# Three feed-forwards that multiply x before its norm's factor is known, with two covered tiles in place of four

## The chip, the cores and the metric

The kernel runs on one core of a Trainium2 chip. The time is that of one execution on the device in microseconds; the number given for a kernel is the median of its runs. Engines: TensorE (PE; its weight loads are listed as PEld), VectorE (DVE), ScalarE (ACT), GpSimd (POOL) and SyncE (SP). DMAs are issued from SP's queue and from POOL's; those of POOL can add what they carry onto what is in the target.

## The reference

A residual stream x of 512 tokens and 1024 features goes through two layers of three parts, each behind an RMS norm:

```python
for l in range(DEPTH):                                   # 2
    x = x + 0.5 * swiglu(rms_norm(x, ffn1_norm[l]), ffn1_w_in[l], ffn1_w_out[l])
    h = rms_norm(x, mix_norm[l]) @ w_mix_in[l]
    ...                                                  # convolution, HGRN2 and FoX heads give y
    x = x + y @ w_mix_out[l]
    x = x + 0.5 * swiglu(rms_norm(x, ffn2_norm[l]), ffn2_w_in[l], ffn2_w_out[l])

def rms_norm(x, gain):
    inv = lax.rsqrt(jnp.mean(x * x, axis=-1, keepdims=True) + EPS)
    return (x * inv) * gain

def swiglu(h, w_in, w_out):
    gate, up = jnp.split(h @ w_in, 2, axis=-1)           # D_FF = 2816 each
    return (jax.nn.silu(gate) * up) @ w_out
```

So there are four feed-forwards, two in each layer. All is float32.

## The kernel before

x is kept transposed (`xT`, 8 tiles of 128 features by 512 tokens), so that the norm's factor `inv` of a token is a row of 512 values, the same on all partitions.

**Three passes a product.** Every matmul takes float32 operands split into a high part (a cast to fp32r on ScalarE) and a low part (the difference, on VectorE): high by high, high by low, low by high (`mm3`, L357, L365, L366). Weights are split the same way in `prepare` (L832 the cast, L834 the subtraction) or, in a plain stream, granule by granule (L343, L344).

**Two ways to a feed-forward's first projection.** The 22 tiles of 128 columns of gate and up are done partly plainly and partly by halves. Plainly: a pair of tiles is four jobs over 8 tiles of features, 96 matmuls of 512 columns. By halves: a unit `("I", w)` of a pair of tiles, w its first, takes 7 products P1 to P7 of sums of halves (24 matmuls of 256 columns each) in place of 8. Products are combined from their PSUM banks: g1, g2 (gate, by halves of the tokens), u2 and the rest (up). `("O", ...)` units do the second projection in the same way, and T the last two tiles. `covered` tells how many tiles are plain: 6 in the first feed-forward (`FIRST`), 4 in the other three.

**What covers what.** While a plain pair runs, the halves are made ready: `enter` (L586) opens the three later feed-forwards. It runs the plain stream of pair 0 on x times the gain (`xh`, `xl`, without `inv`, which multiplies the result later: `clear`), then the norm's matmul (L476) and, on ScalarE, Ln, Exp and Square with a table load behind (L306, L297). Then comes the plain pair 2, and under it the four quarters of x by gain and `inv` (`quarter`, L622, VectorE), the sums of quarters (L645), and their high and low parts (L635, L638, L640).

**The order of the work.** `plan()` writes out the sequence of products (`ORDER_IN` for units of the first projection) and, for each step, the loads of raw weights (SP's queue), the sums of raw weights and the preparation of moving halves. A product's weights are split `LEAD` = 3 products ahead. Four raw tiles of a unit give the weights of seven products; the sums among them are S2 and S3. A sum of two raw tiles is made either by VectorE (`total`) or by a DMA from POOL's queue that adds another tile from DRAM (`add`, L805), or adds the tile S (`add_second`, L860). In the first unit S3 is a VectorE subtraction and the loads, four at first, are issued at L914. Most instructions keep the order in which they are written on their engine, so one that waits holds all behind it.

**The end of the unit.** ScalarE copies a product's bank into SBUF or into another bank, on which later products add: the copy of P1 (L1036), u (L1048), the copy of P6.

## Time and profile before

| | |
|---|---|
| median of 2 runs | 1796.3 us (1795.2 to 1797.4) |
| profiled execution | 1798.4 us, span 1796.6 us |
| TensorE busy | 1787.1 us (99%) |
| VectorE busy | 1493.2 us (83%) |
| ScalarE busy | 1028.0 us (57%) |
| GpSimd busy | 177.3 us (10%) |
| DMA queue of SP (q1) / of POOL (q0) | 182.38 MB, 33.6% / 69.23 MB, 24.0% of 16 engines' span |

The span is the time from the first to the last instruction that the profile shows; the execution's time is a little more. Busy times overlap: TensorE is the engine that hardly ever idles. A row of a timeline begins with the start and the duration in microseconds, then the engine, the line of the kernel, the operation, what it writes and reads, and in brackets the idle time of the engine before it with what ended it.

### The profile page before, as it was taken

Reading aid. Unit: us, or ns where it says so; the run is one execution under the profiler, and the core shown is the slowest. Engines: PE = TensorE matmul, PEld = TensorE weight load, DVE = VectorE, ACT = ScalarE, POOL = GpSimd, SP = SyncE. Lnnn points to the kernel's source line nnn. Section 1 sums busy time; section 2 is a strip of 40 time slices with the busy share of each in tenths; the row PEclk is TensorE's granted clock in tenths of the full one; section 3 lists DMA queues with packets and bytes.
Section 4 is the critical chain, followed back from the end, with each engine's and each line's share of the span. In section 5 each row is a group of like instructions: output and inputs, shape, how many; then the busy total and the mean of one; then the engine's idle time right before and its main releaser. Section 6 shows DMA issues by size and latency. Waiting matters only on the chain.

```text
span 1796.6 us, 35740 instructions
## 1 busy us (share of the span) xinstructions
PE 1787.1 (99%) x14703; PEld 1695.0 (94%) x14703; DVE 1493.2 (83%) x2098; ACT 1028.0 (57%) x1495; POOL 177.3 (10%) x184
## 2 busy tenths in 40 slices
PE   9999999999999999999999999999999999999999
PEld 7899999999888899999989999998998888999998
DVE  8889788876888798879889787997868778888887
ACT  5455555664776465555646555566547755655553
POOL 0002110100000002112001111101000000020110
PEclk9999999999999999999999999999999999999999
DMA  6659685233433857868266786843334346587682
GB/s 199 176 126 195 172 171 149 54 84 84 107 99 108 224 127 169 196 153 185 74 199 133 172 179 166 185 95 77 78 81 114 90 137 168 142 179 197 141 200 71
DMA packets 242083, 254.15 MB, mean 141 GB/s; under 512 B 18904, under 2 KB 224480, under 8 KB 241920
## 3 DMA queue, kind: packets, MB, share of 16 engines
q1 hardware_dynamic: 189424, 182.38, 33.6%
q0 software_dynamic: 52192, 69.23, 24.0%
q8 instruction: 115, 1.88, 0.4%
q14 instruction: 48, 0.39, 0.1%
q10 hardware_dynamic: 304, 0.27, 0.0%
HBM read 221.88 MB, written 2.10 MB: 125 GB/s over the span
## 4 chain that ended last, share of the span: by engine, by line
PE 91%; DVE 4%; DMA 2%; ACT 2%; issue 1%; SPq 0%; POOL 0%; ACTq 0%; POOLq 0%; DVEq 0%
PE mm L357 13%; PE mm L365 13%; PE mm L366 13%; PE pt L365 6%; PE pt L357 6%; PE pt L366 6%; PE sc L365 6%; PE sc L357 6%; PE sc L366 6%; PE po L365 3%; PE po L357 3%; PE po L366 3%; PE po L1770 1%; PE pt L1814 1%; DMA w<-in_ffn_w_out_dram 1%
## 5 line engine op out<-in xcount | busy, mean ns | idle before, releaser
L832 ACT CAST hl<-w 128x1024 fp32r<-128x1024 f32 x354 | 370.7, 1050 | 367.1 <-PE mm L366 97.3
L834 DVE TENSOR_TENSOR hl<-w,hl 128x1024 fp32r<-128x1024 f32 x354 | 430.9, 1220 | 105.2 <-ACT hl L832 104.0
L357 PE MATMUL mm<-xc,hl 128*128 128x256 f32 (+1 forms) x717 | 197.2, 276 | 0.0
L365 PE MATMUL mm<-xc,hl 128*128 128x256 f32 x712 | 197.1, 277 | 0.0
L366 PE MATMUL mm<-xc,hl 128*128 128x256 f32 x712 | 196.9, 277 | 0.0
L344 DVE TENSOR_TENSOR hl<-st,hl 128x512 fp32r<-128x512 f32 (+2 forms) x172 | 133.0, 774 | 62.9 <-ACT hl L343 62.0
L343 ACT CAST hl<-st 128x512 fp32r<-128x512 f32 (+2 forms) x172 | 117.7, 687 | 102.2 <-PE mm L366 43.4
L357 PE MATMUL pt<-xc,hl 128*128 128x256 f32 x514 | 141.4, 276 | 0.0
L365 PE MATMUL pt<-xc,hl 128*128 128x256 f32 x512 | 141.4, 276 | 0.0
L366 PE MATMUL pt<-xc,hl 128*128 128x256 f32 x512 | 141.3, 276 | 0.0
L357 PE MATMUL sc<-xc,hl 128*128 128x256 f32 (+1 forms) x500 | 137.2, 276 | 0.0
L365 PE MATMUL sc<-xc,hl 128*128 128x256 f32 x496 | 137.1, 276 | 0.0
L366 PE MATMUL sc<-xc,hl 128*128 128x256 f32 x496 | 136.9, 276 | 0.0
L357 PEld LDWEIGHTS mm<-xc,hl 128*128 128x128 f32 x717 | 134.6, 188 | 0.2
L366 PEld LDWEIGHTS mm<-xc,hl 128*128 128x128 f32 x712 | 133.7, 188 | 0.0
L365 PEld LDWEIGHTS mm<-xc,hl 128*128 128x128 f32 x712 | 133.7, 188 | 0.0
L365 PE MATMUL mm<-m,hl 128*128 128x256 f32 x416 | 115.0, 277 | 0.0
L357 PE MATMUL mm<-m,hl 128*128 128x256 f32 x416 | 114.8, 276 | 0.0
L366 PE MATMUL mm<-m,hl 128*128 128x256 f32 x416 | 114.8, 276 | 0.0
L357 PE MATMUL mm<-x,hl 128*128 128x512 f32 x272 | 107.7, 396 | 0.0
L365 PE MATMUL mm<-x,hl 128*128 128x512 f32 x272 | 106.3, 391 | 0.0
L366 PE MATMUL mm<-x,hl 128*128 128x512 f32 x272 | 106.2, 390 | 0.0
(529 smaller groups left out, 5781.8 us busy)
## 6 DMA issues: line engine op xcount, KB each, us to landing
w<-in_ffn_w_in_dram SPq DMA_DIRECT2D x140, 512.0 KB, 4.9
w<-in_ffn_w_out_dram SPq DMA_DIRECT2D x88, 512.0 KB, 4.5
w<-in_ffn_w_out_dram POOLq DMA_DIRECT2D x52, 512.0 KB, 7.3
st<-in_w_mix_in_dram SPq DMA_DIRECT2D x88, 256.0 KB, 2.7
w<-S POOLq DMA_DIRECT2D x39, 512.0 KB, 4.8
st<-in_ffn_w_in_dram SPq DMA_DIRECT2D x70, 256.0 KB, 3.3
w<-in_ffn_w_in_dram POOLq DMA_DIRECT2D x35, 512.0 KB, 8.4
st<-in_w_mix_out_dram SPq DMA_DIRECT2D x20, 256.0 KB, 2.7
```

The source lines that it names most:

```text
L343: a = nc.scalar.copy(hi, src[:, c : c + w])
L344: b = nc.vector.tensor_sub(lo, src[:, c : c + w], hi)
L357: i = nc.tensor.matmul(acc[:, c], ah, bh[:, c], start=first and c.start == 0, stop=False, skip_group_check=True,)
L365: nc.tensor.matmul(acc, a, b, start=False, stop=False, skip_group_check=True)
L366: i = nc.tensor.matmul(acc, c, d, start=False, stop=last, skip_group_check=True)
L832: A(nc.scalar.copy(hi, src))
L834: return lambda: V(nc.vector.tensor_sub(lo, src, hi))
L1770: nc.tensor.matmul(self.ob[:, t0 + u * P : t0 + 2 * P], V[:, j, h % 4].rearrange("p a d -> p (a d)"), part[:, j, u:, :].rearrange("p i t - ...
L1814: nc.tensor.transpose(tb[:, j * P : (j + 1) * P], p[:, j * P : (j + 1) * P], self.ident)
```

## The change

In the three later feed-forwards `inv` is no longer part of x's halves.

- `enter` makes the quarters as x times the gain alone (ScalarE, four pieces of 128x256 a quarter). P1, P2 and P3 take the parts `xh`, `xl` that the norm has made anyway; P5, P6, P7 and P4 need sums of quarters ("four sums of x"). Signs of some copies and P1's weights change with it.
- The second covered pair is gone (`COVERED` = 2): a unit of seven products takes its place.
- `inv` multiplies the gate before its Silu (new VectorE products L1084, L1101), and the residual takes the ratio 1/inv: `ratio` (L684), four multiplications of xT at products 14, 16, 18 and 20 (`rescale`), undone in layer 1's mixer (`UNSCALE`, four multiplications) or taken along by the next norm's bias (L694, a ScalarE square) and, at the end of the kernel, by a `column` factor at the output.
- `ORDER_IN` is P1, P5, P6, P2, P7, P3, P4 in all four feed-forwards. S2 is summed in place. S3 of the later units is taken by VectorE only where P7 comes under 4 steps behind P6; else two DMAs add raw tiles from DRAM (0,2 and 2,1) for P7 and P3. The loads of the first unit come in the order 2, 0, 1, 3, the next ones directly behind. Raw tiles and granules get other buffers (`staged`).

```diff
-ORDER_IN = ("P1", "P2", "P6", "P5", "P7", "P3", "P4")
+ORDER_IN = ("P1", "P5", "P6", "P2", "P7", "P3", "P4")
-FIRST = 6
+FIRST, COVERED = 6, 2
...
             if w == covered:
-                when(-1, 6, "adds", u)
-                when(0, 2, "total", u, "S3")
                 continue
+            begin[2] = split["P5"] - AHEAD_SUM - AHEAD_LOAD
+            when(split["P5"] - AHEAD_SUM, 5, "add", u, 2, 3)
+            between(split["P5"], split["P6"] - 1, "total", u, "S2")
+            if split["P7"] - split["P6"] < 4:
+                begin[3] = split["P6"] - AHEAD_LOAD
+                when(split["P6"], 3, "total", u, "S3")
             else:
...
+                when(split["P6"], 4, "add", u, 0, 2)
+            when(split["P6"], 5, "add", u, 2, 1)
...
-        next(second)
-        self.end_norm(nb, fp, parts, True)
...
-                V(nc.vector.scalar_tensor_tensor(
-                    out=t[:, k, :], in0=self.xT[:, i, b * H : (b + 1) * H],
-                    scalar=(self.gain if a == b else self.ngain)[:, i : i + 1],
-                    in1=self.inv[:, b * H : (b + 1) * H], op0=ALU.mult, op1=ALU.mult,
+                A(nc.scalar.activation(
+                    t[:, k, :], self.xT[:, i, b * H : (b + 1) * H], AF.Copy,
+                    scale=(self.gain if a == b else self.ngain)[:, i : i + 1],
                 ))
...
         quarter(0, 0)
-        high("P1")
-        quarter(1, 0)
-        lows["P1"]()
...
         quarter(0, 1)
...
+        add((0, 0), (0, 1))
+        self.end_norm(nb, fp, parts, True)
+        self.table(SILU)
+        next(first, None)
+        high("P5")
         quarter(1, 1)
+        self.given["first"]()
         lows["P5"]()
...
         add((0, 0), (1, 1))
         high("P6")
+        self.given["second"]()
         lows["P6"]()
+        V(nc.vector.scalar_tensor_tensor(out=ratio, in0=nb, ..., in1=self.inv, ...))
...
+        quarter(1, 0)
         next(then)
...
+            0: lambda: (add((0, 1), (1, 1)), both("P7")),
+            1: lambda: (add((0, 0), (1, 0)), high("P4")),
+            2: lambda: lows["P4"](),
+            7: lambda: clear(0),
...
+            14: lambda: rescale(0, 0),
+            16: lambda: rescale(1, 1),
+            18: lambda: rescale(0, 1),
+            20: lambda: rescale(1, 0),
...
+        def first():
+            prepare(*seq[0])()
+
+        def second():
+            prepare(*seq[1])()
+            total(u, "S2")
+            add(u, 0, 2)
```

How the rows stand on the engines at the places where TensorE's first products come from. The first is ScalarE from the norm's last operation on, in layer 0's second feed-forward. Before (`xc` are the high parts of x's halves, `hl<-st` those of the plain pair's weights, `hl<-w` those of the products' weights, `gi` the plain pair's gate):

```order
L306 ACTIVATE nt_7096<-nr_7095 128x512
L297 ACT_TABLE_LOAD
L635 ACTIVATE xc_7143<-xn_7138 128x1024
L343 CAST hl_7179<-st_7176 128x1024
L635 CAST xc_7182<-xn_7146 128x1024
L343 CAST hl_7223<-st_7220 128x1024
L635 CAST xc_7227<-xn_7138 128x1024
L306 ACTIVATE gi_7230<-gi_7230 128x512
L343 CAST hl_7263<-st_7260 128x1024
L635 CAST xc_7291<-xn_7138 128x1024
L832 CAST hl_7297<-w_7131 128x1024
```

All of these but the last stand beside the plain pair's matmuls. Now, at the same place, up to P1's bank (`mm_7161<-mm_7160` is its copy; `w_7057` are P1's raw weights, `w_7054` those of P5 and, summed, P6, `w_7059` those of P2):

```order
L297 ACT_TABLE_LOAD
L641 CAST xc_7123<-xn_7076 128x1024
L629 ACTIVATE xn_7126<-xT,gain_5590 128x256 x4
L863 ACTIVATE hl_7131<-w_7057 128x1024
L641 CAST xc_7136<-xn_7076 128x1024
L863 CAST hl_7139<-w_7054 128x1024
L694 ACTIVATE sqa_7147<-ratio_7145 128x512
L629 ACTIVATE xn_7149<-xT,ngain_7074 128x256 x4
L863 CAST hl_7156<-w_7054 128x1024
L863 CAST hl_7187<-w_7059 128x1024
L1080 ACTIVATE mm_7161<-mm_7160 128x512
```

The weights' casts, which stood at the end of a plain pair, now stand directly behind the table load, between pieces of x, and the copy of P1's bank stands behind the casts for P6 and P2. VectorE at the same place, now, from the norm's factor `inv` on (`hl` are the weights' low parts, of P1, P5, P6, P2 and P7 in this order; `w_7054<-w_7054,w_7057` is S2):

```order
L865 SCALAR_TENSOR_TENSOR hl_7131<-w_7057,hl_7131 128x1024
L646 TENSOR_TENSOR xc_7124<-xn_7076,xc_7123 128x1024
L651 TENSOR_TENSOR xn_7076<-xn_7076,xn_7126 128x1024
L867 TENSOR_TENSOR hl_7139<-w_7054,hl_7139 128x1024
L847 TENSOR_TENSOR w_7054<-w_7054,w_7057 128x1024
L646 TENSOR_TENSOR xc_7137<-xn_7076,xc_7136 128x1024
L684 SCALAR_TENSOR_TENSOR ratio_7145<-po_7073,inv_7093 128x512
L867 TENSOR_TENSOR hl_7156<-w_7054,hl_7156 128x1024
L867 TENSOR_TENSOR hl_7187<-w_7059,hl_7187 128x1024
L651 TENSOR_TENSOR xn_7081<-xn_7081,xn_7126 128x1024
L644 SCALAR_TENSOR_TENSOR xc_7195<-xn_7081,xc_7194 128x1024
L867 TENSOR_TENSOR hl_7223<-w_7057,hl_7223 128x1024
```

Before, four quarters (L622) and granules' low parts (L344) stood here, ahead of the products' weights; now the low parts of x and of weights take turns with the sums of x. The third place is POOL's queue in the same feed-forward, where units of the first and of the second projection alternate (products 75 to 79 of the change's sequence; `in` and `out` in the names tell the projection). Before:

```order
L860 DMA w_9355<-S_9474 128x1024
L805 DMA w_9058<-in_ffn_w_out_dram 128x4x256
L805 DMA w_9188<-in_ffn_w_out_dram 128x4x256
L805 DMA w_9118<-in_ffn_w_out_dram 128x4x256
L805 DMA w_9290<-in_ffn_w_out_dram 128x4x256
```

Now:

```order
L835 DMA w_9375<-in_ffn_w_in_dram 128x4x256
L835 DMA w_9112<-in_ffn_w_out_dram 128x4x256
L835 DMA w_9278<-in_ffn_w_in_dram 128x4x256
L835 DMA w_9243<-in_ffn_w_out_dram 128x4x256
L835 DMA w_9173<-in_ffn_w_out_dram 128x4x256
L835 DMA w_9345<-in_ffn_w_out_dram 128x4x256
```

The add from the tile S is gone here, and the unit of the first projection takes two adds from DRAM (for P7 and for P3) that stand directly among those of the second projection.

## The prediction

> **What bounds the kernel now.** I began with the page: the head, the busy shares and the chain that ended last.

> ```profile
> span 1796.6 us, 35740 instructions
> PE 1787.1 (99%) x14703; PEld 1695.0 (94%) x14703; DVE 1493.2 (83%) x2098; ACT 1028.0 (57%) x1495; POOL 177.3 (10%) x184
> PE 91%; DVE 4%; DMA 2%; ACT 2%; issue 1%; SPq 0%; POOL 0%; ACTq 0%; POOLq 0%; DVEq 0%
> ```

> TensorE is busy for 99% of the span and makes 91% of the chain, so every matmul removed is time removed, as long as TensorE still waits for nobody. How little it waits now is the next view, TensorE's waits by releaser (8 rows, the first and the last):

> ```profile
> PE pt L1814 <- DVE QA L1716: 1.3, 2, 0.6
> ...
> PE po L476 <- ACT sh L467: 0.2, 1, 0.2
> ```

> The eight rows sum to under 6 us, and none has a product of a feed-forward's first unit. Whatever the change adds as a wait is new loss. The third view is the stretch that the change rewrites, here in layer 0's second feed-forward: first the second covered pair, then the seven products of the first unit (columns: PE, PEld, DVE, ACT, POOL busy; clock; DMA share; GB/s).

> ```profile
> 599.58:621.34 21.76, 21.76 (x98) 18.02 (x97) 21.52 (x30) 10.01 (x11) 1.09 (x2) 1.00 0.75 221
> 621.36:640.41 19.05, 19.05 (x170) 19.05 (x169) 17.11 (x19) 12.14 (x14) 1.10 (x1) 1.00 0.55 112
> ```

> In the covered pair VectorE works 21.52 of 21.76 us. That is the making of x's normed halves, their high and low parts and the sums, all under matmuls that don't need them. The change takes that cover away: what VectorE and ScalarE must do between the norm and the first products decides.

> **What is removed and added on TensorE.** A covered pair is 96 matmuls of 512 columns, 21.76 us by the first window; a unit is 168 of 256 columns, 19.05 us by the second (2.72 a product of 24). Each of the three feed-forwards gains 21.76 − 19.05 = 2.71 us; three make **−8.1 us**. This is all that the change can give.

> **What the first products then wait for.** Times are on the clock of this execution. Nothing ahead of the norm's sum is later than now, by the order of the rows: the two pieces of x scaled there take up idle time of ScalarE (4.86 us ahead of the norm's Ln). Timeline of TensorE, ScalarE and VectorE at this place:

> ```profile
> 593.65 0.62 PE L476 MATMUL po<-sh,ones_mean 128*128 128x512 f32 x2
> 599.58 0.39 PE L357 MATMUL mm<-x,hl 128*128 128x512 f32 x1
> 594.32 0.69 ACT L306 ACTIVATE nr<-po,epsc 128x512 f32<-128x512 f32 x1 [4.86 <-PE po L476]
> 596.35 1.28 ACT L297 ACT_TABLE_LOAD   x1
> 599.99 1.06 ACT L635 ACTIVATE xc<-xn 128x1024 fp32r<-128x1024 f32 x1 [2.35 <-DVE xn L622]
> 616.32 1.99 ACT L832 CAST hl<-w 128x1024 fp32r<-128x1024 f32 x2
> 597.55 0.69 DVE L462 TENSOR_TENSOR inv<-nr,nt 128x512 f32<-128x512 f32 x1
> 601.46 1.22 DVE L638 SCALAR_TENSOR_TENSOR xc<-xn,xc 128x1024 fp32r<-128x1024 f32 x1
> 602.59 1.22 DVE L344 TENSOR_TENSOR hl<-st,hl 128x1024 fp32r<-128x1024 f32 x1
> ```

> The norm's sum ends at 594.27, the first pair's last matmuls run until 599.58, and there P1 is now due. ScalarE is free for it only after the table load, at 597.63. A pass over 128x1024 costs ScalarE 1.05 us, 0.95 where one follows another (1.99 for two); VectorE 1.22, or 1.13 (601.46 to 602.59); the group rows of the weights' two passes, quoted next, have the same over 354 each (1050 and 1220 ns). A quarter of x is now four ScalarE pieces of 128x256, which have no row of this line; the nearest are the first three here; behind them are x's sums and the weights' casts and subtractions:

> ```profile
> L1758 ACT ACTIVATE P<-P,rs 128x256 f32<-128x256 f32 x16 | 8.2, 510 | 3.4 <-DVE rs L1756 3.4
> 570.72 0.71 ACT L437 ACTIVATE x<-xT,gain 128x512 fp32r<-128x512 f32 x1
> 571.34 0.62 ACT L453 ACTIVATE sq<-xT 128x512 f32<-128x512 f32 x1
> L645 DVE TENSOR_TENSOR xn<-xn,xn 128x1024 f32<-128x1024 f32 x12 | 14.6, 1216 | 0.0
> L832 ACT CAST hl<-w 128x1024 fp32r<-128x1024 f32 x354 | 370.7, 1050 | 367.1 <-PE mm L366 97.3
> L834 DVE TENSOR_TENSOR hl<-w,hl 128x1024 fp32r<-128x1024 f32 x354 | 430.9, 1220 | 105.2 <-ACT hl L832 104.0
> ```

> A piece is bounded by 0.51 (single, 128x256) and 0.31 (half the 0.62 pitch of 128x512); I take 0.41, so 1.64 a quarter. Both ends move an entry by under 1 us. Now the changed rows, in the order shown above, each engine taking its rows in turn:

> - ScalarE: high part of P5's x to 598.6, quarter (1,1) to 600.2, P1's weights to 601.3. VectorE: their low part to 602.5. **P1** is due at 599.58 and has two matmuls that need high parts alone; it stands 2.7 us and ends at 605.05.
> - VectorE: low part of P5's x to 603.7, the sum for P6 to 604.8. ScalarE: P6's x to 605.9, and only behind it P5's weights, to 606.8. VectorE: their low part to 608.1. **P5** stands 2.8 us and ends at 610.6.
> - VectorE: weight sum 609.2, low part of P6's x 610.4, ratio 611.0. ScalarE: square of the ratio 611.6, quarter (1,0) 613.2, P6's weights 614.2, P2's weights 615.2, and then the copy of P1's bank, which P1 left ten microseconds earlier, 615.7. P6 adds onto that copy. **P6** stands 5.1 us and ends at 618.4. P2 follows without a wait to 621.1.
> - VectorE: low parts of P6's and P2's weights to 616.6, the sum for P7 617.75. ScalarE: P7's x 618.8, P7's weights 619.8, u 620.3. VectorE: both low parts, the sum for P4 to 622.4. ScalarE: P4's x 623.5, and then the copy of P6's bank, 623.95, on which P7 adds. **P7** stands 2.9 us and ends at 626.7; P3 and P4 follow to 632.1.

> Without a wait the unit would end at 599.58 + 19.05 = 618.6: **13.5 us of waits**. In the last feed-forward there is no square and quarter (1,0) isn't behind the ratio, which brings the copies forward: 10.4. Two entries by 13.5 and one by 10.4 make **+37.4 us**. In the units behind, VectorE has 44 us of work, by the same durations, for 18 products of 2.72 (49 us): by the order's rows it keeps up, but nothing wins the waits back, since TensorE is the bound.

> **The loads.** P5's and P6's weights come out of a DMA that adds one tile onto another.

> ```profile
> 592.64 1.37 POOL L805 DMA_DIRECT2D w<-in_ffn_w_in_dram  x1 [58.27 <-DMA w<-in_ffn_w_in_dram]
> w<-in_ffn_w_in_dram POOLq DMA_DIRECT2D x35, 512.0 KB, 8.4
> q0 software_dynamic: 52192, 69.23, 24.0%
> w<-S POOLq DMA_DIRECT2D x39, 512.0 KB, 4.8
> ```

> Issued at 592.64 and landed 8.4 us later, this sum is there at 601.0, ahead of its cast (from 605.9). The loads that are now issued without a wait don't set the end. All four feed-forwards now take S3 by two such adds instead of a VectorE subtraction and an add from a tile. Where units of both projections meet, six adds follow one another within four products (third order extract above). The queue moved 69.23 MB in 24.0% of the span: 0.524 MB in 3.3 us. The fifth add is needed 9 products (24.5 us) later by a weight that takes 1.05 + 1.22 us: 5 × 3.3 + 2.3 = 18.8, in time. By 4.8 each (the row of adds from S) it is 26.3, 1.8 late, 7 us over four feed-forwards; by 8.4 each, one after another, 44.3, some 20 late each, 80. The row of the queue's own time is nearest: I take +2, keep 0 and 7 in the range, and leave the far end to a rival.

> **Small edits.** The sixteen VectorE multiplications of x by a ratio cost some 1.2 us each; idle VectorE (17% of the span) hides them. Uncovered they would be 20 us, too; I take 0, since products 14 to 20 have a free step each. The column factor at the end replaces copies by scaled copies: 0.

> **Sum.** −8.1 + 37.4 + 2 = +31.3 us on the profiled execution (1798.4 us, span 1796.6) gives 1829.7. The median of the runs, 1796.3, is 2.1 lower: **1828 us**, +1.7%. A measurement of this kernel tells from no change about 2%, 1832.2 on this side and 1760.4 on the other.

> **Rivals.**

> *The clock.* TensorE starts at half rate, and at the end no wait is long enough to show whether a pause brings that back:

> ```profile
> 5.55 1.22 PE L1962 MATMUL sc<-x,hl 128*128 128x512 f32 x2
> 6.57 1.05 PE L1962 MATMUL pt<-x,hl 128*128 128x512 f32 x2
> ```

> Two matmuls of 512 columns take 1.05 to 1.22 here and 0.62 at 593.65. If the 5.1 us before P6 lowers the clock, P6 and part of P2 run at double length, 2.7 to 5.4 more, of which P7's wait hides up to 2.9: +2.6 an entry at the most likely, 8 in all, and 1836. [...]

> *Queue late.* With the adds one after another at the far end the time passes 1850; half of it gives 1868. Against it: the queue's own 3.3 us. With the clock both get 0.17, 1834 to 1850 and beyond.

> *The chain is shorter.* If ScalarE's pieces and hand-offs let P5's and P6's waits overlap (a bank's copy done while VectorE still sums), 4 to 8 us an entry remain: 1796.3 − 8.1 + 2 + 3 × (4 to 8) = 1802 to 1814. 0.17.

> *Not slower: the weights' high parts don't stand behind the norm.* P1's and P5's raw weights are there before 601; if their casts and the bank copies found ScalarE free as soon as their inputs are, only VectorE's row would be left, and the order of x's sums would fit beneath P1 to P6. It decides at 2.7 us of waits an entry, a fifth of my sum: then 1788 to 1797. For it: ScalarE idles 4.86 us ahead of the norm. Against it: the rows put each cast behind the table load. 0.06. That the change doesn't do what it says would need matmuls of 512 columns in those places; the order has them gone.

> **How the numbers follow.** Forecast 0.60, its own range 1818 to 1836 (pieces, hand-offs, 0 to 7 for the queue). A quarter of it, 0.14, lies over 1832.2, with the clock and queue 0.31 slower; nothing reaches 1760, 0.01; the rest is within 2%. The range of 8 in 10 goes from 1806 to 1843: it leaves out the not-slower case, the low part of the shorter chain and the late queue.

> **What will show it.** Right: TensorE's waits gain rows at the first unit of three feed-forwards with releasers VectorE (weights' low parts) for P1 and P5, and ScalarE (copies) for P6 and P7, of some 2.7, 2.8, 5.1 and 2.9 us; 288 matmuls of 512 columns fewer, 504 of 256 more; a granted clock of 1.00 in the unit. Wrong: waits at products 80 to 90 on a DMA (queue), rows of 256 columns at twice 0.11 us behind P6's wait (clock), or a unit that takes 19 to 22 us from the last plain matmul to its seventh product (short chain).

## The result, and the profile after

The changed kernel takes 1880.1 us (two runs, 1878.1 and 1882.0) against 1796.3: a ratio of 1.047 (95% interval 1.041 to 1.052). The profiled execution took 1882.0 us, 83.6 more than that of before. From the page, the head, the busy shares and the chain that ended last:

```profile
span 1880.3 us, 36231 instructions
PE 1815.3 (97%) x14919; PEld 1728.0 (92%) x14919; DVE 1509.3 (80%) x2075; ACT 1054.9 (56%) x1554; POOL 212.5 (11%) x202
PE 80%; DVE 8%; ACT 4%; DMA 4%; issue 2%; SPq 0%; ACTq 0%; POOLq 0%; DVEq 0%
```

TensorE no longer makes nine tenths of the chain. Its waits by releaser, which summed to under 6 us, begin now with these rows (engine, line, releaser, us in all, times, longest):

```profile
PE mm L361 <- ACT g L1090: 15.4, 3, 5.5
PE po L361 <- ACT g L1090: 13.4, 3, 5.0
PE mm L361 <- ACT mm L1080: 9.5, 3, 4.6
PE mm L361 <- ACT hl L863: 6.3, 5, 1.6
PE mm L361 <- ACT g L1063: 5.0, 3, 3.5
PE mm L370 <- DVE hl L867: 2.4, 4, 0.8
```

The last four lie in the first unit of the three feed-forwards, where waits were forecast. The first two, the largest, were not forecast: L1090 is the copy of P6's bank in the units behind the first. The windows of the three units of each of the three feed-forwards show how much each takes (its length in us, then busy time of PE, PEld, DVE, ACT, POOL, the granted clock, DMA share, GB/s); without a wait a unit takes 19.05:

```profile
600.54:633.64 33.10, 25.02 (x170) 23.81 (x170) 22.37 (x22) 17.23 (x24) 3.87 (x3) 0.85 0.63 144
633.64:659.77 26.13, 21.63 (x171) 21.43 (x169) 17.03 (x20) 11.22 (x15) 2.58 (x2) 0.87 0.53 121
659.77:686.54 26.77, 22.08 (x171) 21.88 (x170) 17.91 (x21) 9.99 (x12) 2.59 (x2) 0.87 0.51 119
952.57:986.41 33.84, 25.36 (x171) 24.04 (x170) 23.16 (x23) 17.23 (x24) 3.88 (x3) 0.85 0.63 142
986.41:1011.70 25.29, 21.36 (x171) 21.16 (x169) 16.93 (x20) 11.24 (x15) 2.59 (x2) 0.93 0.56 126
1011.70:1038.71 27.01, 21.55 (x170) 21.35 (x169) 17.64 (x21) 9.74 (x12) 2.59 (x2) 0.87 0.52 117
1542.33:1574.15 31.82, 24.26 (x170) 23.08 (x170) 23.16 (x22) 17.14 (x23) 3.89 (x3) 0.89 0.60 144
1574.15:1601.28 27.13, 22.13 (x171) 21.93 (x169) 17.03 (x22) 11.01 (x14) 2.58 (x2) 0.87 0.53 117
1601.28:1628.59 27.31, 22.10 (x171) 21.91 (x170) 18.50 (x21) 10.06 (x13) 2.59 (x2) 0.88 0.52 116
```

The first units sum to 98.8 us, 41.6 over 3 × 19.05. The second and third ones sum to 159.6, 45.3 over 6 × 19.05. With the 8.1 us that the removed pairs give, 41.6 + 45.3 − 8.1 = 78.8 of the 83.6 us. Of the rest 1.3 us is a longer wait on VectorE near the end (2.16 us in place of 0.87), and 1.1 the half clock behind it.

**What P7 waits for in the second unit.** Timelines of TensorE, ScalarE, VectorE, POOL and SP's queue:

```profile
649.18 0.58 PE L361 MATMUL po<-xc,hl 128*128 128x256 f32 x1 [4.50 <-ACT g L1090]
649.57 0.41 PE L369 MATMUL po<-xc,hl 128*128 128x256 f32 x1
642.37 0.59 ACT L1093 ACTIVATE u<-mm 128x512 f32<-128x512 f32 x1
647.59 1.04 ACT L863 CAST hl<-w 128x1024 fp32r<-128x1024 f32 x1 [4.63 <-DMA w<-in_ffn_w_in_dram]
648.54 0.59 ACT L1090 ACTIVATE g<-po 128x512 f32<-128x512 f32 x1
637.90 1.22 DVE L847 TENSOR_TENSOR w<-w,w 128x1024 f32<-128x1024 f32 x1
639.66 2.58 POOL L835 DMA_DIRECT2D w<-in_ffn_w_in_dram  x2 [20.22 <-DVE w L847]
640.28 10.01 SPq L832 DMA_DIRECT2D w<-in_ffn_w_in_dram  x3
```

Read backwards: P7 adds onto P6's bank, which ScalarE has to copy away first (648.54). The copy stands behind the cast of P3's weights (647.59), and that cast waits 4.63 us for a DMA: the add of a raw tile onto S2. POOL issues it at 639.66, as soon as VectorE's difference for P7 (L847) has read the tile, beside loads on SP's queue, and it lands 7.9 us later.

**The clock.** The matmuls at 649.57 start 0.21 us apart, twice the 0.113 (19.05 over 168) of before. The granted clock changes in steps of 3.41 us; these are some of the windows (length, PE busy, granted clock, DMA share, GB/s):

```profile
599.48:602.89 3.41, 1.83 (x9) 1.00 1.14 289
602.89:606.31 3.42, 2.81 (x13) 0.50 1.09 384
606.31:609.72 3.41, 3.22 (x15) 0.50 1.03 319
609.72:613.13 3.41, 2.48 (x22) 1.00 0.12 13
951.05:954.47 3.42, 1.98 (x11) 1.00 1.17 237
954.47:957.88 3.41, 2.76 (x24) 1.00 1.09 369
643.85:647.27 3.42, 0.83 (x8) 1.00 1.21 200
647.27:650.68 3.41, 1.50 (x7) 0.50 1.17 236
650.68:654.09 3.41, 3.41 (x18) 0.50 0.76 236
654.09:657.50 3.41, 3.41 (x31) 1.00 0.35 122
```

After 1.6 us of idling in one window (599.48) the next two are granted half the clock; after 2.6 (643.85) two again; after 1.4 (951.05) none. Over the whole execution matmuls of 256 columns under half clock take 27.8 us more than at full clock, against 0 before. P7 of the second and third units takes 5.1 to 5.3 us in five of the six cases and 4.5 in the other, in place of 2.7: of the 45.3 us, 30 are waits and 15 the half clock.

### The profile page after: what moved, and what is told of

Read it like the earlier page. It is cut to its first block, busy times and chain, and to the rows that moved or that the text cites. A ratio compares the mean times of both kernels' runs of the same rounds, so it can differ in the third digit from the quotient of the medians.

```text
span 1880.3 us, 36231 instructions
## 1 busy us (share of the span) xinstructions
PE 1815.3 (97%) x14919; PEld 1728.0 (92%) x14919; DVE 1509.3 (80%) x2075; ACT 1054.9 (56%) x1554; POOL 212.5 (11%) x202
## 4 chain that ended last, share of the span: by engine, by line
PE 80%; DVE 8%; ACT 4%; DMA 4%; issue 2%; SPq 0%; ACTq 0%; POOLq 0%; DVEq 0%
PE mm L361 14%; PE mm L369 14%; PE mm L370 14%; PE pt L369 4%; PE pt L370 4%; PE pt L361 4%; PE sc L361 4%; PE sc L370 4%; PE sc L369 4%; DMA w<-in_ffn_w_in_dram 4%; PE po L361 3%; PE po L370 3%; PE po L369 3%; DVE hl L867 2%; DVE w L847 1%
## 5 line engine op out<-in xcount | busy, mean ns | idle before, releaser
L863 ACT CAST hl<-w 128x1024 fp32r<-128x1024 f32 x380 | 397.7, 1050 | 425.5 <-PE mm L370 103.1
L867 DVE TENSOR_TENSOR hl<-w,hl 128x1024 fp32r<-128x1024 f32 x380 | 462.1, 1222 | 160.3 <-ACT hl L863 159.5
L361 PE MATMUL mm<-xc,hl 128*128 128x256 f32 (+1 forms) x1090 | 309.5, 284 | 31.7 <-ACT g L1090 15.4
L370 PE MATMUL mm<-xc,hl 128*128 128x256 f32 x1088 | 308.0, 283 | 2.4 <-DVE hl L867 2.4
L369 PE MATMUL mm<-xc,hl 128*128 128x256 f32 x1088 | 307.5, 283 | 0.0
L361 PEld LDWEIGHTS mm<-xc,hl 128*128 128x128 f32 x1090 | 211.3, 194 | 34.6 <-ACT g L1090 15.9
L361 PE MATMUL mm<-x,hl 128*128 128x256 f32 (+2 forms) x761 | 235.7, 312 | 4.5 <-ACT hl L863 4.5
L370 PE MATMUL mm<-x,hl 128*128 128x256 f32 (+1 forms) x752 | 233.4, 310 | 2.0 <-DVE hl L865 2.0
L369 PE MATMUL mm<-x,hl 128*128 128x256 f32 (+1 forms) x752 | 233.5, 310 | 0.0
L835 POOL DMA_DIRECT2D w<-in_ffn_w_in_dram x88 | 113.9, 1403 | 936.3 <-DVE w L847 254.0
L370 PEld LDWEIGHTS mm<-xc,hl 128*128 128x128 f32 x1088 | 211.0, 194 | 3.4 <-DVE hl L867 3.4
L369 PEld LDWEIGHTS mm<-xc,hl 128*128 128x128 f32 x1088 | 211.3, 194 | 0.0
L347 ACT CAST hl<-st 128x512 fp32r<-128x512 f32 (+2 forms) x160 | 105.2, 660 | 96.3 <-PE mm L370 45.0
L361 PEld LDWEIGHTS mm<-x,hl 128*128 128x128 f32 x761 | 145.1, 192 | 12.7 <-ACT hl L863 5.8
L370 PEld LDWEIGHTS mm<-x,hl 128*128 128x128 f32 x752 | 143.5, 191 | 10.6 <-DVE hl L865 2.6
L369 PE MATMUL pt<-m,hl 128*128 128x256 f32 x544 | 151.4, 278 | 1.7 <-DVE m L799 1.5
L370 PE MATMUL pt<-m,hl 128*128 128x256 f32 x544 | 151.0, 278 | 0.0
L361 PE MATMUL pt<-m,hl 128*128 128x256 f32 x544 | 151.0, 278 | 0.0
L369 PEld LDWEIGHTS mm<-x,hl 128*128 128x128 f32 x752 | 143.9, 191 | 6.9
L370 PE MATMUL sc<-m,hl 128*128 128x256 f32 x480 | 132.7, 277 | 0.0
L361 PE MATMUL sc<-m,hl 128*128 128x256 f32 x480 | 132.6, 276 | 0.0
## 6 DMA issues: line engine op xcount, KB each, us to landing
w<-in_ffn_w_in_dram SPq DMA_DIRECT2D x152, 512.0 KB, 5.7
w<-in_ffn_w_in_dram POOLq DMA_DIRECT2D x88, 512.0 KB, 8.1
w<-in_ffn_w_out_dram SPq DMA_DIRECT2D x88, 512.0 KB, 6.6
w<-in_ffn_w_out_dram POOLq DMA_DIRECT2D x52, 512.0 KB, 8.2
```

The source lines that it names most:

```text
L347: a = nc.scalar.copy(hi, src[:, c : c + w])
L361: i = nc.tensor.matmul(acc[:, c], ah, bh[:, c], start=first and c.start == 0, stop=False, skip_group_check=True,)
L369: nc.tensor.matmul(acc, a, b, start=False, stop=False, skip_group_check=True)
L370: i = nc.tensor.matmul(acc, c, d, start=False, stop=last, skip_group_check=True)
L835: G(nc.gpsimd.dma_start(raw[u, q], src(u, q2), accum_op=ALU.add))
L863: A(nc.scalar.activation(hi, src, AF.Copy, scale=-1.0) if other else nc.scalar.copy(hi, src))
```

## The experiments

Each run is compared with runs of the kernel before on the same chip; the changed kernel's ratio is 1.047 (1.041 to 1.052), and 0.01 is 18 us. A gain is the difference of two ratios.

**Banks copied ahead of the casts.**

```diff
+            if kind == "I" and p == "P1":
+                A(nc.scalar.activation(work[u, "c"], acc, AF.Copy, scale=-1.0))
+            elif kind == "I" and p == "P6" and (u, "g2") not in work:
+                ...                                  # the copy of P6's bank
             rest = prepare(*seq[n + LEAD]) if n + LEAD < len(seq) else None
```

> The changed kernel; in units of the first projection ScalarE copies the banks of P1 and P6 before, not after, it casts the weights for three products later. Theory A (in the second and third unit of the three feed-forwards P7 waits for the copy of P6's bank, which stands on ScalarE behind the cast of P3's weights, and that cast waits for a DMA that adds a raw tile): P7 starts at once, and P3 waits instead for its weights' high and low parts, 1 to 2.3 us. Each of the six waits of 3.9 to 5.5 us shrinks by about 2.6, and the half clock behind it (1.5 to 2.9 us a unit) goes for the most part: 6 x (2.6 + 2.3) = 29 us, 1851 us. Theory B (P7 waits for something of its own, its weights or its bank): no change, 1880.

Measured: 1873.9 us, 1.043 (1.042 to 1.045): 6 us gained, not 29, and the interval overlaps that of the changed kernel. In the profiles the six units are together 9.6 us shorter. ScalarE, and TensorE's largest wait:

```profile
642.89 0.59 ACT L1068 ACTIVATE g<-po 128x512 f32<-128x512 f32 x1
648.26 2.00 ACT L863 CAST hl<-w 128x1024 fp32r<-128x1024 f32 x2 [4.78 <-DMA w<-in_ffn_w_in_dram]
PE mm L361 <- ACT hl L863: 18.5, 10, 3.9
```

The copy now runs at 642.89 and P7 starts at once, so it was the copy that P7 waited for. But the cast waits as long as before, and everything behind it with it: P3 waits instead in all six units (0.6 to 3.9 us for that cast, 0.8 for the low part), and P4 for 0.9 us in three. The order on ScalarE moved most of the wait; it did not make it.

**The add left out.**

```diff
-            when(split["P6"], 5, "add", u, 2, 1)
+            if w - covered > 4 or covered > 2:
+                when(split["P6"], 5, "add", u, 2, 1)
```

> The changed kernel without the DMA add that makes P3's weights in the second and third unit of the three later feed-forwards (the weights of P3 lack a tile there). Theory A (that add lands late and holds ScalarE, and P7 behind it): the six waits of 28.7 us in all go, and with them the half clock behind them, 15 us: 1836 us. Theory B (ScalarE and VectorE are simply behind in their own rows there): P7's weights and copy would come as late as before, under 10 us gained, above 1870.

Measured: 1841.2 us, 1.025 (1.023 to 1.026): 39 us gained. The second unit of the same feed-forward, from the windows:

```profile
633.05:652.41 19.36, 19.36 (x170) 19.36 (x170) 16.33 (x20) 10.93 (x14) 1.28 (x1) 1.00 0.53 127
```

It takes 19.4 us at full clock in place of 26.1. VectorE and ScalarE are not behind by themselves: the add is what these units wait for.

**The wait filled with matmuls.**

```diff
+            if self.raw and kind == "I" and p == "P2" and w in (covered + 2, covered + 4):
+                again = parts[u, p]
+                product(u, p, acc, False, False, False)          # once more
+                ...
+                product(u, p, acc, False, False, False, 1)       # and half of it
+                ...
```

> The changed kernel; in the second and third unit of the three later feed-forwards the matmuls of P2 run two and a half times in place of once (36 more matmuls, 4.1 us, so P2's product counts two and a half times), which fills the wait before P7 with work. Theory C (a pause of over 1.5 us in a window of 3.4 us halves the clock, and that is a cost of its own beside the wait): TensorE's granted clock stays at 1.0 in those units, P7 runs in 2.7 us in place of 5.3, and 10 to 15 us are gained although 216 matmuls are added: 1865 to 1870 us. Theory D (the half clock costs nothing, since the next thing is late anyway): 1880 or more.

Measured: 1874.7 us, 1.044 (1.041 to 1.047), with 216 matmuls more than the changed kernel.

```profile
640.00:660.00 20.00, 19.59 (x169) 1.00 0.73 159
```

The granted clock stays at 1.00 where it was 0.50, and P7 takes 2.9 us (it starts at 651.27 and P3 at 654.12). So P7 does in five of the six units; in the last one TensorE still waits 2.6 us and P7 takes 4.5. In the profiles the nine units are together 9.7 us shorter, although the 24.5 us of added matmuls (216 × 0.113) are 2 us more than they took from the waits (28.8 to 6.5 us): 12 us, near the 15 that the product times give. Of the whole time only 5 us are gained, and the interval overlaps that of the changed kernel. So the clock has a price of its own, as theory C has it; its size rests on the profiles.

**The norm behind the first three parts.**

```diff
-        self.end_norm(nb, fp, parts, True)
-        self.table(SILU)
         next(first, None)
         high("P5")
...
         lows["P6"]()
+        self.end_norm(nb, fp, parts, True)
+        self.table(SILU)
```

> The changed kernel with the norm's chain (Ln, Exp, Square, table load, inv) behind the parts for P1, P5 and P6 on ScalarE and VectorE, not ahead of them; these parts need only x and the weights. Theory E (the first unit's waits are the rows of ScalarE and VectorE that start only when the norm and the table load are done): P1's wait of 1.5 to 2.2 us and P5's go; P6 still waits some 5 us for the copy of P1's bank, since the norm's rows now stand ahead of it, but its copy comes some 5 us sooner, as does all behind it: 3 x 5.4 = 16 us, 1864 us. Theory F (the first unit waits for DMA adds, landed only after 600): under 4 us gained, 1876 or more.

Measured: 1870.8 us, 1.042 (1.040 to 1.044): 8 us gained, between the two theories. The interval overlaps that of the changed kernel, but in the profiles, too, the three first units are together 8.0 us shorter and the six others 0.3 longer. P1 starts without a wait and P5 waits 0.8 to 1.9 us, but P6 waits 6.8, 7.5 and 3.4 us (expected: some 5), and the mean granted clock of the run stays at 0.983, beside the 0.982 of the changed kernel. The norm's rows hold P1 and P5, as theory E has it; moved, the norm's chain holds P6 instead.

**VectorE's sum in place of the add.**

```diff
-            when(split["P6"], 5, "add", u, 2, 1)
+            if split["P7"] - split["P6"] < 4:
+                when(split["P6"] + 1, 3, "total", u, "S5")       # q(2) + q(1)
+            else:
+                when(split["P6"], 5, "add", u, 2, 1)
```

> The changed kernel; in the second and third unit of the three later feed-forwards VectorE adds the raw tile for P3's weights (1.2 us, both tiles are in SBUF) in place of a DMA. Theory A (the DMA add's landing holds the unit): the same waits go as without the add, 1841 us, plus at most 6 x 1.2 for VectorE's sums: 1841 to 1848 us. Theory B (VectorE, 17 of 19 us busy there, is the next bound): the sums push its rows past TensorE's, and waits of 1 us and more come back in these units: 1850 to 1860 us.

Measured: 1843.3 us, 1.027 (1.026 to 1.029): 35 us gained, with no part of the sum left out. The six units take 19.0 to 20.4 us. One sum of 1.2 us does what a DMA of 7.9 us did.

**A quarter of the add's bytes.**

```diff
+                G(nc.gpsimd.dma_start(raw[u, q][:, :1], src(u, q2)[:, :1], accum_op=ALU.add))
```

> The changed kernel in which the DMA add for P3's weights in the second and third unit of the three later feed-forwards carries a quarter of its tile (128 KB in place of 512; three quarters of that sum are left out). Theory G (the add is late because its bytes share the DMA engines with the loads that are issued beside it): it lands in some 4 us in place of 7.9, the six waits before P7 shrink from 4.8 to about 1, and the half clock behind them goes: 6 x (3.8 + 2.5) = 38 us, 1842 us. Theory H (it is late because it is issued late, behind VectorE's difference for P7, and a DMA of any size takes as long to start): it lands in 6 us or more, waits of 3 us stay and with them the half clock in part, 1865 us or more.

Measured: 1848.4 us, 1.028 (1.025 to 1.030): 34 us gained. The row of its issues (KB each, median us to landing):

```profile
w<-in_ffn_w_in_dram POOLq DMA_DIRECT2D x6, 128.0 KB, 4.2
```

It lands in 4.2 us, issued no earlier (640.11), and the waits before P7 shrink to 2.1 us at most. The bytes beside the loads make it late, theory G. How much of it is its own bytes and how much the loads beside it was not parted.

**The first unit's rows in other orders.** With VectorE's sum and the copies ahead, the norm's chain went behind P1:

```diff
+            0: lambda: (norm(), (add((0, 1), (1, 1)), both("P7"))),
```

> As the kernel with VectorE's sum, and besides: banks copied ahead of casts, and the norm's Ln, Exp, Square, table load and inv behind the first product (the norm's matmuls stay), ratio and square behind the fourth. Theory E (the first unit's waits are the rows that start behind the norm and the copy behind casts): P1's and P5's waits go, P6's shrinks under 1 us, P7 waits some 2 us for the copy of P6's bank; the waits of 9 us an entry and 4 us of half clock become 3 us: 1843 - 3 x 10 = 1813 us. Theory F (DMA adds bound the first unit): P5 to P7 still wait 5 us and more an entry, 1830 or above.

Measured: 1839.6 us, 1.025 (1.023 to 1.026), not 1813. P1's wait went and P6's is under 1 us, but P7 waits 5.0 to 5.9 us in place of 2: the norm's rows and the sum behind them hold the copy of P6's bank. Next, P7's weights by VectorE:

```diff
+            if self.raw:
+                total(u, "S3")
```

> As the last one, and P7's weights of the first unit are a VectorE difference of tiles in SBUF in place of a DMA add. Theory E: P7's weights are ready by some 4 us sooner, which brings ScalarE's rows and the copy of P6's bank forward by up to 2 us: 0 to 6 us in all, 1807 to 1813 us. If instead VectorE's extra 1.2 us ahead of P6's weights is what TensorE waits for: 3 x 1.2 = 4 us slower, 1817 us.

Measured: 1837.3 us, 1.024 (1.022 to 1.025); P7 still waits 4.8 us in all three. Then the norm where both engines idled, and P4's part behind the copy:

```diff
         add((0, 0), (1, 1))
+        self.end_norm(nb, fp, (), True)
+        self.table(SILU)
         high("P6")
...
+            2: lambda: high("P4"),
+            3: lambda: lows["P4"](),
```

> As the last kernel, but the norm's Ln, Exp, Square, table load and inv stand ahead of the high part of P6's x, where ScalarE idled 3.7 us for VectorE's sum and VectorE 4.4 us for a DMA; and the high part of P4's x stands behind the copy of P6's bank, not ahead of it. Theory E (rows, not data, set the first unit's waits): P7's wait of 4.8 us in each of the three entries and the 2.7 us of half clock behind it go: 3 x 7.5 = 22 us, 1815 us; what is left is some 2 us an entry at P5 and P6. If P7 waits for something that no row order moves: 1837 as before.

Measured: 1826.0 us, 1.015 (1.012 to 1.018): 16 us gained by the ratios, where 22 were expected. In the first units P7 waits no more; they take 24.2 to 25.0 us in place of 30.4 to 31.1. Two things moved here at once, and which of them freed P7 was not parted. At last P5's sum by VectorE:

```diff
+            if self.raw:
+                total(u, "S1")                       # q(2) + q(3)
```

> As the last one, and the first unit's sum for P5's weights is VectorE's, of tiles loaded in the order 2, 0, 3, 1, in place of a DMA add that landed at 602.6, 11 us behind its issue. If that landing sets P5's and P6's remaining waits of some 2 us: 3 x 1.5 to 2 = 5 us, 1810 us. If VectorE's rows do: no change, 1815 us.

Measured: 1818.4 us, 1.011 (1.009 to 1.013): 7 us gained, as if the landing set those waits. Its three units in the first entry:

```profile
599.50:622.58 23.08, 20.74 (x170) 19.93 (x169) 20.48 (x21) 14.13 (x20) 4.01 (x3) 1.00 0.72 155
622.58:643.23 20.65, 19.64 (x170) 19.28 (x169) 16.84 (x20) 10.99 (x15) 1.28 (x1) 1.00 0.43 102
643.23:663.11 19.88, 19.80 (x170) 19.28 (x169) 19.80 (x22) 10.10 (x12) 1.27 (x1) 1.00 0.42 134
```

The clock is whole and no wait of TensorE in them is longer than 1 us, yet a first unit takes 4 to 5 us more than 19.05. That is more than the 2.7 us that the removed pair gives, and no version tried beats the kernel before. VectorE is busy for 20.5 of the 23.1 us; that it is what holds the unit now was not tested.

## Why the prediction was wrong

**The saving: not measured by itself.** The sum from the windows closes with −8.1 us to within 5 of the 83.6.

**The first unit: the sum right, its parts not.** Forecast 37.4 us over three entries, measured 41.6: 14.1, 14.8 and 12.8 against 13.5, 13.5 and 10.4. The forecast was made of waits alone. Measured were 24.1 us of waits and 17.5 of products that took longer, 11.8 of these by the half clock, which the sum had at 0; the granted clock was 0.85 to 0.89 where 1.00 was forecast. What the walk had right is when ScalarE and VectorE are done with their rows:

```profile
606.82 1.04 ACT L863 CAST hl<-w 128x1024 fp32r<-128x1024 f32 x1
616.16 0.58 ACT L1080 ACTIVATE mm<-mm 128x512 f32<-128x512 f32 x1
```

They came some 1 us behind the walk, about as much as the norm's sum itself was later (595.2 in place of 594.3): P5's weights cast at 607.9 (606.8), the copy of P1's bank done at 616.7 (615.7), P4 over at 633.6 (632.1). These rows set when a product can start, so most waits came shorter than forecast and the products before them longer: P1 and P5 at half clock ended nearer to when the next thing was ready. The runs that moved the rows (the norm late, and the last four) moved these waits with them, as the walk has it. No run held the clock up in the first unit, so that its half clock was mostly hidden there is argued from the row times and not shown; so far as it was not hidden, the sum came near by luck.

**The units behind: the step that failed.** "It keeps up", said the walk, and set 0 us; measured were 45.3. The step weighed VectorE's work alone and found it enough, which the run without the add confirms. It left out that these units, too, take P3's weights from a DMA add. It wrote that all four feed-forwards now take S3 by two adds. By the change's own rule the second and third unit, whose P7 stands two products behind P6, keep VectorE's difference, and the add for P3 has to wait until that difference has read the tile. The prediction did look at adds, and quoted that one takes 8.4 us to land; but it asked only whether six of them in a row fit at products 75 to 79, at 3.3 us each, and took +2 for all. In the units behind the first, one add has to come in the 3.3 us between its issue (639.66, behind VectorE's difference) and ScalarE's readiness for the cast (642.96). The latency of one, in a row that was on the page, decided, and not the queue's throughput. At 7.9 us that is 4.6 late; the forecast's own 8.4 would have given 5.1, six times over.

**The clock: right as a rival, too small and too rare.** It was priced at 8 us for one wait an entry with 0.17 for it and the queue together. In the nine units the clock fell twelve times, for six or seven windows an entry, and six of these falls stand behind the add that was not seen. Half clock cost 27.8 us in the whole execution, 15 of them in the second and third units. The forecast asked it of a wait of 5.1 us alone; measured, 1.6 us idle in a window of 3.41 (599.48) had two windows at 0.50 behind it, and 1.00 came back behind a window without idling (650.68).

**The queue: no wait found.** Behind the three units of each of the three feed-forwards, where units of both projections meet, TensorE waits for no DMA, and for VectorE 1.2 us at most up to the wait at the very end named below; the +2 us has no row.

**The rival on the other side and the shorter chain: refuted for this kernel.** Reordered by hand (the last version) the first unit loses 4 to 5 us an entry in place of 14, near the 4 to 8 of the shorter chain; as written it does not.

**Small edits.** VectorE's multiplications by the ratio stayed hidden, as forecast; at the very end one wait for VectorE grew from 0.87 to 2.16 us, and among the rows ahead of it stands the gate's new multiplication (0.69 us). No run tested whether it is the cause.

## What to carry to other kernels

Before covered work is removed, walk what it hid up to the last DMA: for each transfer that an edit puts into a unit, take the time from issue to landing in a row with the same traffic and hold it against the time from its earliest issue to the first instruction in order that reads its target. A throughput that fits says nothing about one transfer that is waited for. And price with a wait of TensorE the half-clock windows that came behind it: here one wait of 2.16 us had one behind it (1859.00 to 1862.41), and in the second and third units they cost half as much again as the waits (15 us beside 30).

## What the runs showed of the hardware

Beside that, products of 24 matmuls ran for stretches of 50 us at 0.118 us a matmul in place of 0.113 at a granted clock of 1.00, from 748 to 802 in the changed kernel and in the kernel before, too (1043 to 1096). By these two numbers such a stretch lost some 2 us, an estimate; its cause was not looked for.
